# Clearing semaphores ahead of the final wait of a transfer-bound kernel, and letting that wait subtract

## Chip, cores, metric

The kernel runs on one core of one Trainium2 chip. The metric is the device time of one execution in microseconds (us). Each kernel was also executed once under the profiler, which leaves a trace. The *span* is the time from the first to the last instruction of that trace, and the measured time of the same execution is a little longer.

## The reference

```python
def reference(x, y):               # both 1024 x 4096, float32
    z = x * y
    return (0.5 * z * (1 + np.tanh(np.sqrt(2 / np.pi) * (z + 0.044715 * z ** 3)))).astype(np.float32)
```

A product and a GELU, element by element. 33.55 MB come in and 16.78 MB go out, so there are 50.33 MB to move for two passes of arithmetic.

## The kernel before

Everything is laid out as 128 partitions x 32768 columns. VectorE multiplies in place in `xs`, ScalarE applies the GELU in place, and the Sync engine (SP) issues all seven transfers and closes the program. Only this closing part is changed.

```python
    sem_x = [nc.alloc_semaphore(f"sem_x{i}") for i in range(len(X_LOADS))]    # 2
    sem_y = [nc.alloc_semaphore(f"sem_y{i}") for i in range(len(Y_LOADS))]    # 3
    sem_o = [nc.alloc_semaphore(f"sem_o{i}") for i in range(len(STORES))]     # 2
    sem_mul = nc.alloc_semaphore("sem_mul")
    sem_act = nc.alloc_semaphore("sem_act")
    # ... (loads, multiplications, activations cut)
    for i, (a, b) in enumerate(STORES):                # (0, 16384), (16384, 32768)
        nc.sync.wait_ge(sem_act, b // STEP)
        nc.sync.dma_start(out=out_r[:, a:b], in_=xs[:, a:b]).then_inc(sem_o[i], 16)
    for i in range(len(STORES)):
        nc.sync.wait_ge(sem_o[i], 16)
    nums = sorted(s.num for s in [*sem_x, *sem_y, *sem_o, sem_mul, sem_act])
    assert nums == list(range(nums[0], nums[-1] + 1))
    nc.sync.sem_clear(range(nums[0], nums[-1] + 1))
```

A *semaphore* is a counter: a transfer or an engine raises it, and a wait holds an engine until it has reached a value. The clear puts all nine back to zero at once, so that the next execution can count from there, and before the change it comes after both waits.

Of the kernel before, what the change touches and what calls it, by code (L numbers as in the profile page):

```python
# [1 line left out]

# [4 lines left out]


F32 = mybir.dt.float32
GELU = mybir.ActivationFunctionType.Gelu_apprx_tanh  # L10


X_LOADS = [(0, 16384), (16384, 32768)]

Y_LOADS = [(0, 16384, 0), (16384, 24576, 0), (24576, 32768, 8192)]
STEP = 4096
STORES = [(0, 16384), (16384, 32768)]
Y_RING = 16384


def _hoist(nc, issued):

    here = nc.cur_bb.bb.instructions
    first = nc.main_func.blocks[0].instructions
    for ins in issued:
        del here[next(k for k, i in enumerate(here) if i is ins or i.name == ins.name)]
    engine = issued[0].engine
    at = next(
        k
        for k, i in enumerate(first)  # L30
        if i.engine == engine and type(i).__name__ == "InstDrain"
    )
    first[at:at] = issued


@with_exitstack
def kernel(
    ctx: ExitStack,
    tc: tile.TileContext,
    x: bass.AP,  # L40
    y: bass.AP,
    out: bass.AP,
):
    nc = tc.nc
    P = nc.NUM_PARTITIONS

    x_r = x.flatten_outer_dims().rearrange("(p a) c -> p (a c)", p=P)
    y_r = y.flatten_outer_dims().rearrange("(p a) c -> p (a c)", p=P)
    out_r = out.flatten_outer_dims().rearrange("(p a) c -> p (a c)", p=P)
    total_f = x_r.shape[1]  # L50


    tc.close()
    tc.compile()  # L54

    xs = nc.alloc_sbuf_tensor("xs", [P, total_f], F32).ap()
    ys = nc.alloc_sbuf_tensor("ys", [P, Y_RING], F32).ap()
    sem_x = [nc.alloc_semaphore(f"sem_x{i}") for i in range(len(X_LOADS))]
    sem_y = [nc.alloc_semaphore(f"sem_y{i}") for i in range(len(Y_LOADS))]
    sem_o = [nc.alloc_semaphore(f"sem_o{i}") for i in range(len(STORES))]  # L60
    sem_mul = nc.alloc_semaphore("sem_mul")
    sem_act = nc.alloc_semaphore("sem_act")

    def load_x(i):
        a, b = X_LOADS[i]
        return nc.sync.dma_start(out=xs[:, a:b], in_=x_r[:, a:b]).then_inc(sem_x[i], 16)  # L66

    def load_y(i):
        a, b, r = Y_LOADS[i]
        return nc.sync.dma_start(  # L70
            out=ys[:, r : r + b - a], in_=y_r[:, a:b]
        ).then_inc(sem_y[i], 16)

    _hoist(nc, [load_x(0).ins, load_y(0).ins])
    load_x(1)
    for i in (1, 2):
        nc.sync.wait_ge(sem_mul, (Y_LOADS[i][1] - Y_LOADS[1][0]) // STEP)
        load_y(i)

    n = 0  # L80
    for i, (a, b, r) in enumerate(Y_LOADS):
        for j, (xa, xb) in enumerate(X_LOADS):
            if xa <= a < xb:
                nc.vector.wait_ge(sem_x[j], 16)
        nc.vector.wait_ge(sem_y[i], 16)  # L85
        for c in range(a, b, STEP):
            nc.vector.tensor_mul(  # L87
                out=xs[:, c : c + STEP],
                in0=xs[:, c : c + STEP],
                in1=ys[:, r + c - a : r + c - a + STEP],  # L90
            ).then_inc(sem_mul, 1)
            n += 1
            nc.scalar.wait_ge(sem_mul, n)
            nc.scalar.activation(  # L94
                out=xs[:, c : c + STEP], in_=xs[:, c : c + STEP], func=GELU
            ).then_inc(sem_act, 1)

    for i, (a, b) in enumerate(STORES):
        nc.sync.wait_ge(sem_act, b // STEP)
        nc.sync.dma_start(out=out_r[:, a:b], in_=xs[:, a:b]).then_inc(sem_o[i], 16)  # L100
    for i in range(len(STORES)):
        nc.sync.wait_ge(sem_o[i], 16)
    nums = sorted(s.num for s in [*sem_x, *sem_y, *sem_o, sem_mul, sem_act])
    assert nums == list(range(nums[0], nums[-1] + 1))
    nc.sync.sem_clear(range(nums[0], nums[-1] + 1))


# [1 line left out]
_INS = ['x', 'y']  # L109
_OUTS = [((1024, 4096), 'float32')]  # L110


# [23 lines left out]
```

## Time and profile before

| | before |
|---|---|
| measured, first three runs | 120.77 to 120.79 us, median 120.79 |
| measured, the profiled execution | 120.85 us |
| its span | 119.535 us |
| measured minus span, same execution | 1.315 us |
| last increment of the last store's semaphore | 119.415 us |
| from there to the end of the span (the **tail**) | 0.120 us |

Values with three decimals are from the single records of the trace; the views round them to one or two.

The prediction below shows the views that carry the argument. One more belongs here: the busy times of the kernel before by stage. The columns are the stretch, its length, the busy us of VectorE, ScalarE and POOL with the number of instructions, the granted clock, the busy share of the DMA engines and GB/s.

```profile
58.80:80.80 22.00, 8.76 (x2) 8.77 (x3) 0.00 (x0) 1.00 1.03 429
80.80:93.30 12.50, 8.76 (x2) 9.31 (x3) 0.00 (x0) 1.00 0.97 419
93.30:119.50 26.20, 0.00 (x0) 0.00 (x0) 0.00 (x0) 1.00 0.92 400
```

The last row: no engine computes for 26.2 us and only the two stores run (the first lands at 100.1 us, the last at 119.4). Whatever the Sync engine does in that stretch *before* the last store has landed lies beside it. Whatever it does *after* is added.

### The profile page before, as it was taken

The numbers are of one execution on the slowest core, as the hardware profiler recorded it, in microseconds if no ns is written. First come the engines' busy times: TensorE is split into PE (matmuls) and PEld (weight loads), VectorE is DVE, ScalarE is ACT, GpSimd is POOL, SyncE is SP. The second block draws the span as 40 slices with busy tenths as digits, with TensorE's granted clock in tenths as the row PEclk, the third lists the DMA queues.
The fourth block names the chain that finished last, engine by engine and source line by source line (L and its number), as shares of the span: only waits on it lengthen the run. The fifth ranks groups of instructions, "written<-read, shape, count | busy, mean of one in ns | idle before, by whom it ended". The sixth has DMA issues, their size and how long they took to land.

```text
span 119.5 us, 68 instructions
## 1 busy us (share of the span) xinstructions
DVE 35.0 (29%) x8; ACT 30.2 (25%) x9; POOL 0.2 (0%) x4
## 2 busy tenths in 40 slices
DVE  0000000000000199999600049959990000000000
ACT  3000000000000006797780000977479200000000
POOL 0000000000000000000000000000000000000000
DMA  9889888998899889988898989998899888988890
GB/s 351 351 373 680 351 351 351 636 417 351 351 636 417 351 351 526 526 351 351 351 526 351 504 373 482 395 526 351 351 395 658 351 351 351 702 351 351 351 680 22
DMA packets 1008, 50.33 MB, mean 421 GB/s; under 512 B 112, under 2 KB 112, under 8 KB 112
## 3 DMA queue, kind: packets, MB, share of 16 engines
q1 hardware_dynamic: 1008, 50.33, 98.5%
HBM read 33.55 MB, written 16.78 MB: 421 GB/s over the span
## 4 chain that ended last, share of the span: by engine, by line
DMA 53%; DVE 22%; ACT 3%; SPq 0%; issue 0%; DVEq 0%
DMA ys<-in_y_dram 53%; DVE xs L87 22%; ACT xs L94 3%; SPq L66 0%; DVEq L85 0%
## 5 line engine op out<-in xcount | busy, mean ns | idle before, releaser
L87 DVE TENSOR_TENSOR xs<-xs,ys 128x4096 f32<-128x4096 f32 x8 | 35.0, 4421 | 54.7 <-DMA ys<-in_y_dram 54.7
L94 ACT ACTIVATE xs<-xs 128x4096 f32<-128x4096 f32 x8 | 28.9, 3617 | 61.1 <-DVE xs L87 61.1
L94 ACT ACT_TABLE_LOAD x1 | 1.3, 1283 | 1.9 <-PEq L54 1.9
L120 POOL MEMSET const-bfloat16-1.0<- 128x1 bf16 x1 | 0.1, 102 | 0.0
L120 POOL MEMSET const-uint8-127<- 128x1 uint8 x1 | 0.1, 102 | 0.0
L120 POOL MEMSET const-float32-1.0<- 128x1 f32 x1 | 0.1, 99 | 0.0
L120 POOL MEMSET const-float32-0.0<- 128x1 f32 x1 | 0.1, 98 | 0.2 <-issue 0.2
## 6 DMA issues: line engine op xcount, KB each, us to landing
ys<-in_y_dram SPq DMA_DIRECT2D x2, 4096.0 KB, 21.1
xs<-in_x_dram SPq DMA_DIRECT2D x2, 40.3
out_dram<-xs SPq DMA_DIRECT2D x2, 31.9
ys<-in_y_dram SPq DMA_DIRECT2D x1, 40.8
```

The lines of the kernel that those rows point to most:

```text
L87: nc.vector.tensor_mul(out=xs[:, c : c + STEP], in0=xs[:, c : c + STEP], in1=ys[:, r + c - a : r + c - a + STEP],).then_inc(sem_mul, 1)
L94: nc.scalar.activation(out=xs[:, c : c + STEP], in_=xs[:, c : c + STEP], func=GELU).then_inc(sem_act, 1)
L120: nc = _bacc.Bacc("TRN2", target_bir_lowering=False, num_devices=1)
```

## The change

Its intent is to have less left to do when the last store lands: clear the eight semaphores that are done with while that store still runs, and let the final wait put its own semaphore back to zero.

```diff
-    sem_o = [nc.alloc_semaphore(f"sem_o{i}") for i in range(len(STORES))]
     sem_mul = nc.alloc_semaphore("sem_mul")
     sem_act = nc.alloc_semaphore("sem_act")
+    sem_o = [nc.alloc_semaphore(f"sem_o{i}") for i in range(len(STORES))]
@@
-    for i in range(len(STORES)):
+    for i in range(len(STORES) - 1):
         nc.sync.wait_ge(sem_o[i], 16)
-    nums = sorted(s.num for s in [*sem_x, *sem_y, *sem_o, sem_mul, sem_act])
+    nums = sorted(s.num for s in [*sem_x, *sem_y, *sem_o[:-1], sem_mul, sem_act])
     assert nums == list(range(nums[0], nums[-1] + 1))
     nc.sync.sem_clear(range(nums[0], nums[-1] + 1))
+    nc.sync.wait_ge(sem_o[-1], 16).then_inc(sem_o[-1], -16)
```

The compiled program has two closing instructions either way. Before: a wait for the second store, then a clear of nine that also carries the wait for the first store. After: a clear of eight that carries the wait for the first store, then one wait for the second store with a subtraction of 16.

## The prediction

> **What bounds the kernel now.** I read the page first, then the chain that ended last in order of time, then the waits of the DMA queue on the Sync engine (SP), and last the two closing lines of the kernel one by one, because they are all that the change touches.
>
> The page says that transfers fill the span. In part 2 the DMA row stands at 8 or 9 in every slice but the last, and in part 3 one queue holds 16 DMA engines for 98.5% of the span. VectorE (29%) and ScalarE (25%) have room to spare.
>
> ```profile
> span 119.5 us, 68 instructions
> ...
> DVE  0000000000000199999600049959990000000000
> ACT  3000000000000006797780000977479200000000
> ...
> DMA  9889888998899889988898989998899888988890
> ...
> q1 hardware_dynamic: 1008, 50.33, 98.5%
> ```
>
> Here 50.33 MB in 119.5 us is 421 GB/s. VectorE and ScalarE have their last 9 in slice 30 or 31, about 90 us in; from there to the end the kernel is one store draining.
>
> The chain by time agrees: loads, multiplications, loads, multiplications, and a last activation that ends at 89.68 + 3.62 = 93.30 us. Its printed end is that last piece of computing, not the end of the span, so a second view is needed for the remaining 26.2 us. The waits of the Sync queue fill it:
>
> ```profile
> engine line waited for: us in total, times, longest us
> SPq L70 <- DVE xs L87: 56.2, 2, 47.9
> SPq L100 <- ACT xs L94: 33.8, 2, 30.5
> SPq L102 <- DMA out_dram<-xs: 25.8, 1, 25.8
> ```
>
> The third line is the one to see: the wait of line 102 sits for 25.8 us on the last store and is over only with it. What comes after that wait is on the path of everything, and it is two instructions:
>
> ```profile
> L102 SPq EVENT_SEMAPHORE  x1: 17/17/17, 119.4 to 119.4; - x1
> ...
> L105 SPq EVENT_SEMAPHORE_RANGE_CLEAR  x1: 40/40/40, 119.5 to 119.5; - x1
> ```
>
> The columns are shortest, middle and longest duration in ns, then the start in us. The records of the trace behind these lines carry three decimals: the sixteenth and last increment of the last store's semaphore is at 119.415 us, the wait of line 102 starts at 119.431 and lasts 0.017, the clear starts at 119.495 and lasts 0.040, and that is the end of the span, 119.535 us. So from the landing to the end of the span there are 0.120 us, and nothing else is in them. That is the whole stake of this change.
>
> **What the Trainium skill says.** "Perfetto Trace Analysis", section "Sequencer-only Instruction (DRAIN, etc)": the profiler reports only the execution of such an instruction; its wait for a semaphore and the spreading of its own update are not in the reported window. The trace agrees: line 102 is printed as 17 ns though it waited 25.8 us. So I work with starts and not with durations alone: the step from the wait to the clear is 119.495 - 119.431 = 0.064 us, of which only 0.017 is printed.
>
> "DMA: Bandwidth & Descriptors", section "Why a DMA increments its semaphore by 16 and not by 1": each engine that takes part adds 1 after its own data, and only the full 16 means that all has landed. The trace has 16 increments of the last store's semaphore, from 118.962 to 119.415 us. So subtracting 16 at that moment leaves exactly zero, what the clear left before, and the increments cannot be cut across by the early clear, since that semaphore is now outside its range.
>
> The same page, section "Anatomy of one DMA — SWDGE (gpsimd) path", puts most of the fixed cost of a transfer (about 2 us there, for the other way of issuing) into waiting for the confirmation of the write. Here the last data packet ends at 119.065 and the last increment comes at 119.415, 0.35 us later. That is much less than the page's figure, and in any case the change leaves it as it is.
>
> "Runtime: NRT & Kernel Launch", section "The ~15µs preamble/postamble breakdown", lists work of the runtime after the kernel. No record of the trace shows any of it; I only see that the measured 120.79 us is about 1.25 us more than the span of 119.535, and I assume that this part follows the end of the Sync engine and keeps its size.
>
> **The change part by part.** (1) The first wait loop loses its last turn. The compiled instruction lists show that the wait for the first store never was an instruction of its own: before, it rides on the clear. After, it still rides on the clear, which now stands alone in front. Instructions removed: none; SP has 7 listed rows in both.
>
> (2) The clear moves ahead of the final wait. It now starts when the first store has landed. That store was issued at 62.45 us and took 37.7 us (the longer of the two landing times of line 100), so 62.45 + 37.7 = about 100.1 us. All loads, multiplications and activations are over by then (last activation 93.30, last store issued 93.3), so nobody needs the eight semaphores any more. Its 0.040 us lie inside the 25.8 us of waiting for the second store, with 119.4 - 100.1 = 19.3 us of slack. Cost on the path: zero.
>
> (3) The final wait gains a subtraction. Waits with a subtraction are already in the trace: two of POOL's four in line 54, and POOL's first in line 120. They are printed as 17 ns, the same as the bare wait of line 102:
>
> ```profile
> L54 POOLq EVENT_SEMAPHORE  x4: 17/17/17, 1.4 to 1.8; - x4
> ```
>
> In its records POOL's wait with subtraction starts at 1.073 us and the next instruction at 1.152, a step of 0.079 against 0.064 from the bare wait to the clear. So the update may cost 0.015 us after the printed window.
>
> (4) The semaphores are allocated in another order (the stores' last), so that the range to clear stays contiguous without the last one; the clear then covers 8 instead of 9. It costs nothing on the path either way.
>
> Sum for the span: landing 119.415, start of the final wait 0.016 later as before, 0.017 of execution, end at 119.448 instead of 119.535. That is **0.087 us** less, which is the 0.064 step to the clear plus its 0.040 minus the 0.017 that the wait itself still takes. For the measured time I take off the 0.015 of a slower step after a subtraction: 0.087 - 0.015 = 0.072, and the middle of the two is 0.08. 120.79 - 0.08 = **120.71 us**, 0.07% faster.
>
> **The rivals.** *The saving vanishes behind the end of the program.* If the 1.25 us outside the span wait for something other than SP's last instruction, or start at the landing anyway, the time stays 120.79. For it: I cannot see that stretch. Against it: the other four engines have nothing recorded after 93.30 us, so they cannot be the late ones. About 1 in 5.
>
> *The clear costs more than it prints.* Clearing nine semaphores may hold the sequencer beyond the 0.040 us, just as the bare wait occupied 0.064 for a printed 0.017. Then the saving is larger: if the clear's step exceeds its window by the same 0.047, 0.064 + 0.087 - 0.079 = 0.072 by steps, and every further hidden 0.05 would come on top, giving about 120.62 to 120.66. About 1 in 5.
>
> *The subtraction is dear.* A read-modify-write of a semaphore that DMA engines have just written might be slower than POOL's in the preamble. Twice the 0.079 step would bring the time back to 120.79. I see nothing for it beyond the 0.015; 1 in 10.
>
> *The transfers shift.* A clear at 100 us, in the middle of the last store, could disturb it only if it touched that store's semaphore, which it does not. The stream itself may wander: the three timed runs lie within 0.02 us, but the profiled execution took 120.85. This gives the range its width and not the middle.
>
> **Range and chances.** The middle is 120.71. Below it the second rival reaches about 120.62; above it the first and third end at 120.79; a shift of the stream of a few hundredths, as between 120.79 and 120.85, widens both ends: 120.60 to 120.82. A change of 2% would be 2.4 us, and all that follows the last landing inside the span is 0.12 us, so a faster verdict would need twenty times the stake. Slower by 2% would need a disturbed stream. Chances: faster 0.003, same 0.992, slower 0.005.
>
> **What the profile of the changed kernel would show.** The clear of the Sync queue at about 100.1 us, 40 ns or slightly less, and no line of it at the end; the last Sync instruction is the wait, 17 ns, some 0.016 us after the last landing, and the span ends with it, near 119.45 us; the landing of the last store is unmoved near 119.4; engine work and DMA rows are the same. If the span falls by 0.09 and the measured time does not, the first rival is right. If the wait prints clearly more than 17 ns, the third. The prediction would be wrong if the landing of the last store itself moved by more than a tenth of a microsecond, or if the unseen end of the program grew or shrank with what SP does last.

## The result, and the profile after

| | before | after |
|---|---|---|
| median of six runs each, taken together | 120.87 us | 120.78 us |
| lowest to highest | 120.77 to 121.28 | 120.63 to 121.05 |
| ratio | | 0.999, 95% interval 0.997 to 1.001: the same |
| span of the profiled execution | 119.535 | 119.297 |
| last increment of the last store | 119.415 | 119.264 |
| tail | **0.120** | **0.033** |
| measured minus span, same execution | 1.315 | 1.333 |

A ratio is the mean time of one kernel's fast runs over the mean of the other's in the same rounds, so it is not quite the ratio of the medians quoted beside it.

The page of the changed kernel gives the same picture of transfers as before. These are its span, its DMA row and its DMA queue:

```profile
span 119.3 us, 68 instructions
...
DMA  9899888998899889988898989998889888998894
...
q1 hardware_dynamic: 1008, 50.33, 98.7%
```

The two closing lines of the changed kernel, each from the view of one source line (shortest, middle and longest duration in ns, then the start):

```profile
L105 SPq EVENT_SEMAPHORE_RANGE_CLEAR  x1: 45/45/45, 100.0 to 100.0; - x1
...
L106 SPq EVENT_SEMAPHORE  x1: 17/17/17, 119.3 to 119.3; - x1
```

The clear has left the end: it starts at 100.0 us, when the first store has landed. The last instruction is the wait, and it prints 17 ns with its subtraction, as the bare one did.

The waits of the Sync queue of the changed kernel hold a trap for readers:

```profile
SPq L100 <- ACT xs L94: 33.7, 2, 30.4
SPq L106 <- SPq L106: 19.3, 1, 19.3
SPq L105 <- DMA out_dram<-xs: 6.5, 1, 6.5
```

The 25.8 us before the end are now cut in two by the clear, 6.5 + 19.3 = 25.8. But the second part is put down to line 106 itself. The releaser is inferred from semaphore events, and the last event on this semaphore is now the subtraction of line 106. What really released it is the store: its sixteenth increment is at 119.264 us and the wait starts at 119.280. A wait that names itself is to be checked against the landings.

The span fell by 0.238 us, but only 0.120 - 0.033 = 0.087 of it belongs to the tail. The other 0.151 is the landing of the last store, 119.415 against 119.264. It was there before any changed instruction ran: the last load already landed 0.148 earlier, at 80.641 against 80.789 us. The repeats below show that this wanders.

### The profile page after: what moved, and what is told of

Read it like the earlier page. It is cut to its first block, busy times and chain, and to the rows that moved or that the text cites. A ratio compares the mean times of both kernels' runs of the same rounds, so it can differ in the third digit from the quotient of the medians.

```text
span 119.3 us, 68 instructions
## 1 busy us (share of the span) xinstructions
DVE 35.0 (29%) x8; ACT 30.2 (25%) x9; POOL 0.2 (0%) x4
## 4 chain that ended last, share of the span: by engine, by line
DMA 53%; DVE 22%; ACT 3%; SPq 0%; issue 0%; DVEq 0%
DMA ys<-in_y_dram 53%; DVE xs L87 22%; ACT xs L94 3%; SPq L66 0%; DVEq L85 0%
```

## The experiments

The theory: the stake is the time that the Sync engine needs after the last landing, and each of its instructions there counts in full. The rivals: the end of the program hides it; a clear or a subtraction costs more than it prints; clears beside a running store disturb it. Eleven runs were made, each on one chip and with runs of the kernel before beside it.

### The same two kernels again

No edit; five rounds each.

> The changed kernel once more, with more rounds. Theory: the tail from the last landing to the end of the span is 0.033 us again (0.120 in the kernel before), and the measured time lies 0.07 to 0.09 us below the kernel before, but single runs wander by 0.2 us with the landing of the last store, so the median may differ by anything from -0.3 to +0.15. Rival (the end of the program takes the saving back): measured time minus span is 0.087 us larger than in the kernel before (1.40 against 1.315). If the theory holds it is larger by at most 0.02.

> The kernel before against itself, to measure the noise. Ratio 1.000 with an interval about as wide as that of the change (0.997 to 1.001); tail 0.120 us; measured time minus span 1.315 us.

> The changed kernel a third time. Theory: tail 0.033 us, measured time minus span 1.33 to 1.34, that is 0.01 to 0.02 above the kernel before; measured time 0.07 below before, with single runs scattered over 0.4 us. Pooled over its three rounds of measuring the difference should come out between 0.0 and 0.2 us below before.

| | median | lowest to highest | ratio to before, 95% interval | landing | tail | measured - span |
|---|---|---|---|---|---|---|
| before again | 121.17 | 120.72 to 121.62 | 1.0012, 0.9992 to 1.0033 | 119.407 | 0.120 | 1.323 |
| after again | 120.80 | 120.61 to 121.02 | 0.9982, 0.9969 to 0.9995 | 119.238 | 0.034 | 1.338 |
| after, third time | 120.76 | 120.70 to 120.91 | 0.9991, 0.9978 to 1.0004 | 119.328 | 0.033 | 1.339 |

The tail repeats to 0.001 us, while the time of one and the same kernel wanders by 0.9 us from lowest to highest, ten times the effect. Measured minus span came out slightly above what was expected: 1.323 for 1.315, and 1.338 where at most 0.02 over the kernel before was allowed (0.023 over the first trace of it, 0.015 over the one of the same lot). With all runs of both kernels pooled, before has a mean of 120.96 us (43 runs, standard deviation 0.20) and after 120.81 (17 runs, 0.15). The difference is 0.155 us, with a standard error of 0.046 (the root of 0.20 squared over 43 plus 0.15 squared over 17), so 0.06 to 0.25. The 0.087 of the tail lies inside. The timed runs thus speak for a small gain but do not size it; the trace does.

The records also say where the wandering comes from: not from the closing part. In the 13 traces the last load lands anywhere between 80.617 and 81.193 us, but from there to the landing of the last store it is 38.610 to 38.636 us in eleven of them (the other two are taken up below). Counted from the landing of the last load, the span ends after 38.746, 38.750 and 38.749 us with the old closing (before, before again, and the renumbering below) and after 38.656, 38.655 and 38.665 with the new one, 0.090 less. The measured time of the same six executions, counted from the same point, is 40.061, 40.073 and 40.067 against 39.989, 39.993 and 40.004, 0.072 less.

### The renumbering alone

```diff
 # the kernel before
-    sem_o = [...]          # ahead of sem_mul and sem_act
+    sem_o = [...]          # behind them
```

> The kernel before with only the part of the change that allocates the stores' semaphores last. All theories: tail 0.120 us, measured time minus span 1.31 to 1.33, measured time that of the kernel before within noise (ratio 0.998 to 1.002).

Ratio 1.0007 (0.9991 to 1.0024), tail 0.120 us. The order of allocation is worth nothing in itself. Its profiled execution had its last store land at 119.822 us, 0.4 later than in the first trace of the kernel before: another look at how much the landing wanders without cause in the closing code (its last load had landed 0.404 later, too).

### Only the order of the two waits

```diff
 # the kernel before
-    for i in range(len(STORES)):
+    for i in reversed(range(len(STORES))):
         nc.sync.wait_ge(sem_o[i], 16)
```

> The kernel before with only the order of its two final waits turned round, so that the wait for the last store rides on the clear and the wait for the first store stands alone ahead. Theory: what matters is how many instructions stand behind the last landing: now one, a clear of 0.040 us, so the tail is 0.016 + 0.040 = 0.056 us, 0.064 less than before and 0.023 more than in the changed kernel. Rival (a clear must come after a wait of its own, or a wait on a clear reacts later): the tail stays near 0.12. Measured time 0.06 below before, within the noise of 0.2.

The two closing lines of this kernel, from the views of their source lines:

```profile
L102 SPq EVENT_SEMAPHORE  x1: 17/17/17, 100.1 to 100.1; - x1
...
L105 SPq EVENT_SEMAPHORE_RANGE_CLEAR  x1: 40/40/40, 119.4 to 119.4; - x1
```

The separate wait is now over at 100.1 us, and the clear itself waits for the last store. The tail is 0.056 us, 0.064 less than before, as the theory had it to the thousandth: what went is the step from a wait to the instruction behind it. Measured 120.90 us against 120.88, ratio 1.0004 (0.9992 to 1.0017), within the noise. So 0.064 of the 0.087 in the tail needs no subtraction and no second group of semaphores, only the order in which two waits are written.

### The subtraction undone

```diff
 # the changed kernel
-    nc.sync.wait_ge(sem_o[-1], 16).then_inc(sem_o[-1], -16)
+    nc.sync.wait_ge(sem_o[-1], 16)
+    nc.sync.sem_clear(range(sem_o[-1].num, sem_o[-1].num + 1))
```

> The changed kernel with the subtraction undone: the final wait is bare and a clear of that one semaphore follows, on which the wait rides. Theory: tail 0.016 plus one clear, 0.05 to 0.06 us, whether it clears one semaphore or nine. Rival (a clear's time goes with the number of semaphores): clearly below 0.040 for one semaphore, tail under 0.045. Measured time within noise of the changed kernel.

The wait rides on the clear of the one semaphore, so that again one instruction is left at the end:

```profile
L107 SPq EVENT_SEMAPHORE_RANGE_CLEAR  x1: 25/25/25, 119.6 to 119.6; - x1
```

The tail is 0.042 us, under the 0.05 to 0.06 of the theory, which missed here; the rival had it right. A clear of one semaphore prints 25 ns where the clear of nine at the end of the kernel before prints 40. That the time goes with the number is not shown, though: the early clear of eight prints 45, and an early clear of four, in the kernels with 64 waits below, 43. Measured 120.88 us, ratio 0.9995 (0.9981 to 1.0009). Of the 0.087, the subtraction itself is worth 0.042 - 0.033 = 0.009 over the next best closing. In the measured time counted from the last load's landing that does not show: 39.987 us here and 39.999 for the swapped waits, against 39.989 to 40.004 for the changed kernel.

### Many clears behind the end

```diff
 # the kernel before
-    nc.sync.sem_clear(range(nums[0], nums[-1] + 1))
+    for _ in range(1 + 64):
+        nc.sync.sem_clear(range(nums[0], nums[-1] + 1))
```

> The kernel before with 64 more clears behind its own. Theory: each clear is a step of 0.04 (its printed time) to 0.09 us (0.040 and the 0.047 by which a wait's step exceeds its printed time), all of it behind the landing and all of it in the measured time: 2.6 to 5.8 us more, in the span and in the measured time alike, 123.4 to 126.6 us. Rival (the end of the program hides what SP does last): the span grows by that much, the measured time by 1.3 us less. Rival (a clear costs much more than it prints): steps over 0.1 us, more than 6.4 us.

```profile
L106 SPq EVENT_SEMAPHORE_RANGE_CLEAR  x65: 38/38/63, 119.6 to 124.4; - x65
```

The tail grew from 0.120 to 4.956 us, by 4.836; the measured median went from 121.00 to 125.78, by 4.78 (by 4.85 for the profiled execution, counted from the last load's landing). Measured minus span was 1.338 us. **What the Sync engine does behind the last landing is paid in full**: the rival in which the end of the program takes it back is out. In the records, one clear follows the other at 0.068 us in the steady run of them, for a printed 0.038. The first two steps are 0.089 and 0.080, the last two 0.110 and 0.475. These last two return in other runs and are taken up below.

### Many subtracting waits behind the end

```diff
 # the changed kernel; sem_x and two of sem_y are taken out of the early clear
     nc.sync.wait_ge(sem_o[-1], 16).then_inc(sem_o[-1], -16)
+    four = [*sem_x, *sem_y[:2]]
+    for k in range(16):
+        for s in four:
+            nc.sync.wait_ge(s, 16 - k).then_inc(s, -1)
```

> The changed kernel with 64 more waits behind its last, each of them satisfied and subtracting 1 from a load's semaphore. Theory: a step of 0.079 us each, as POOL's in the preamble, so 5.1 us more than the changed kernel, in the span and in the measured time alike. Rival (subtraction is free behind the printed window): 0.064 us each, 4.1 us. Rival (subtraction is dear): over 0.1 us each, more than 6.4 us.

```profile
L110 SPq EVENT_SEMAPHORE  x64: 17/17/17, 119.8 to 124.4; - x64
```

The tail was 4.733 us, 4.700 more than in the changed kernel, and the measured median 125.62 against 120.88 for the kernel before. The steady step is 0.067 us, less than the 0.079 expected. Sixty-four such steps are 4.29 us, near the lower expectation, and the same two long steps at the end, here 0.104 and 0.441, add the other 0.41. So a subtraction is not dear. What it adds to a steady step is not shown, since no run has a row of bare waits. The step right behind the long wait, from the subtracting final wait to the first of the 64, is 0.088, against 0.064 from the bare wait to the clear in the kernel before.

### Many clears, and many waits, ahead of the final wait

```diff
 # the changed kernel
-    nc.sync.sem_clear(range(nums[0], nums[-1] + 1))
+    for _ in range(1 + 64):
+        nc.sync.sem_clear(range(nums[0], nums[-1] + 1))
```

> The changed kernel with 64 more clears ahead of the final wait. Theory: they lie in the 19.3 us of slack and cost nothing: same time as the changed kernel within 0.2 us, tail 0.033 us, landing of the last store at 119.2 to 119.5. Rival (clears beside a running store disturb it): the landing comes later by a microsecond or more.

This missed. The median was 121.70 us against 121.00 for the kernel before (ratio 1.0058, 1.0045 to 1.0071) and 120.80 for the changed kernel, 0.9 us more for work that should be hidden. The clears themselves did lie in the slack (100.5 to 104.9 us) and the tail was 0.034 as ever; the landing of the last store had moved, to 120.439 us. The page of this kernel has a line in its part 3 that none of the pages above has:

```profile
q1 hardware_dynamic: 1008, 50.33, 97.9%
q14 instruction: 1, 0.01, 0.0%
```

One packet of an instruction queue, 8,192 bytes, runs at 109.721 us for 0.309 us, in the middle of the store. The steps of the clears may mark where it was asked for: 0.110 instead of 0.069 at the last of them, at 104.9 us. That made two theories, told apart by half as many clears, and by as many instructions that are not clears.

```diff
-    for _ in range(1 + 64):                                # 64 clears
+    for _ in range(1 + 32):                                # shadow_32
```

```diff
 # the changed kernel: the 64 subtracting waits of the last experiment, ahead of the final wait   (shadow_waits)
+    for k in range(16):
+        for s in four:
+            nc.sync.wait_ge(s, 16 - k).then_inc(s, -1)
     nc.sync.wait_ge(sem_o[-1], 16).then_inc(sem_o[-1], -16)
```

> The changed kernel with 32 instead of 64 more clears ahead of the final wait. The 64 made the time 0.9 us longer against expectation. Theory A (the clears disturb the running store): half as many clears, half of it, about 0.45 us over the changed kernel. Theory B (the longer program makes the Sync engine fetch instructions once more, as one extra packet of an instruction queue at 109.7 us in that trace, in the middle of the store; the steps of 0.11 us near the last clears mark the place): 32 do not reach that place, no such packet, and the time is that of the changed kernel within 0.2 us.

> The changed kernel with 64 satisfied waits (each subtracting 1 from a load's semaphore) in place of the 64 clears ahead of the final wait. Theory A (clears disturb): no extra clears, so the time of the changed kernel within 0.2 us. Theory B (instruction fetch): the program is as long as with 64 clears, so one packet of the instruction queue during the store, and 0.5 to 1.2 us more.

| ahead of the final wait | measured | instruction packet in the store | issue of last store to landing | tail |
|---|---|---|---|---|
| 1 clear (after, third time) | 120.76 | none | 26.1 | 0.033 |
| 33 clears | 120.76 | none | 26.1 | 0.034 |
| 64 subtracting waits and 1 clear | 121.33 | one, at 109.329 | 26.5 | 0.033 |
| 65 clears | 121.70 | one, at 109.721 | 26.8 | 0.034 |

The first three rows were measured in one lot, the fourth in an earlier one. The landing times are the shortest of the two stores in the view of the issuing line. For 33 clears, 64 waits and 65 clears these are:

```profile
DMA to landing us min/median/max: 26.1/31.9/37.8
```

```profile
DMA to landing us min/median/max: 26.5/32.2/38.0
```

```profile
DMA to landing us min/median/max: 26.8/32.4/38.1
```

Thirty-two more clears cost nothing in time. Sixty-four further instructions of either kind do, and both times one instruction packet runs in the store. In the two kernels with as many instructions *behind* the end, the packet comes at 125.0 us, after the store, and the store lands at 119.486 and 119.669, within what the others show. So the length of the program alone does not make the loss.

Neither theory is the whole of it, as the single packets of the store show. Its data packets carry 65,536 bytes, and in the ten traces without extra instructions ahead of the final wait every one of them that starts after 93.0 us lasts 2.418 us; the early clear of the changed kernel lengthens none. In the three kernels with extra instructions, longer packets appear on one of the 16 DMA engines and on no other. (The trace does not name the engine; it is told by each packet starting where the one before it ended, to 0.004 us.) How much later that engine ended its part of the store, in us:

| ahead of the final wait | by longer store packets, nearly all while the instructions ran | by the instruction packet (0.309) and the longer packet right behind it (0.27) | together | its head start on the last of the other engines | left over |
|---|---|---|---|---|---|
| 33 clears | 0.30 | none | 0.30 | 0.59 | nothing |
| 64 subtracting waits and 1 clear | 0.14 | 0.58 | 0.72 | 0.45 | 0.27 |
| 65 clears | 0.67 | 0.58 | 1.25 | 0.67 | 0.58 |

The head start is what the engine would have had without the delays. So clears beside a running store do slow it, about in proportion to their number, as theory A had it; but they slow one engine, and 33 of them stay within its head start. The instruction packet of theory B runs on that same engine, and with it the head start is used up. The last increment of the store then came 0.467 and 0.471 us after the last data packet, against 0.331 to 0.351 in the other eleven traces. With that, the landing is 0.39 and 0.71 us late, counted from the last load's landing (39.011 and 39.339 us against 38.610 to 38.636).

The Trainium skill ("Runtime: NRT & Kernel Launch", section "Instruction fetch mechanics") describes how each sequencer, the part of an engine that runs its instructions, fetches them in blocks of 16 KiB by transfers of its own, and calls the cost of crossing a block boundary "mostly hidden". The trace agrees that there is such a transfer, though the packet has 8,192 bytes and that a boundary is crossed here is inferred. The cost is hidden from the sequencer, which is waiting anyway, but not from the store: in a kernel whose DMA engines are the bound the time was 0.57 us (121.33 against 120.76) and 0.90 us (121.70 against 120.80) longer, of which the fetch is a part.

What stays open: the remaining 0.2 us between the landings of the profiled executions and these medians; why the instructions slow one DMA engine (the profiler's own recording of them is not excluded); and whether the long steps near the end of each run of 64 belong to that fetch. The first of them, 0.104 to 0.110, ends at the 65th closing instruction in all four kernels; the second, 0.441 and 0.475, at the 66th in two, and in the other two the 66th is the final wait, which hides it.

## Why the prediction was right or wrong

**What bounds the kernel and what is at stake: right.** The transfers are unchanged, and all that the change could touch was the 0.120 us tail. The repeats with 0.120 and the 64 clears that were paid in full both show it.

**Parts 1 to 3, the cost on the path: right.** The prediction had the wait starting 0.016 us after the landing and lasting 0.017, and 0.087 us less behind the landing. The trace has 0.016, 0.017 and 0.087, three times over to 0.001. The span itself ended at 119.297 and not at 119.448, because the landing moved. The early clear was free, as said; it started at 100.0 us (said: about 100.1), but printed 45 ns where "40 ns or slightly less" was forecast. The renumbering, part 4, was free as well.

**The 0.015 for a slower step after a subtraction: supported, not settled.** Measured minus span is 1.333, 1.338 and 1.339 for the changed kernel against 1.315, 1.323 and 1.318 for the three traces with the old closing, on average 0.018 more. An estimate from steps, that is from start to start, says the same. The step behind the very last instruction is not recorded, so it is taken from the rows of 64: the old closing takes 0.064 + 0.068 and the new one 0.067 with steady steps, 0.064 + 0.089 and 0.088 with the steps right behind a long wait, so 0.065 us less either way and not 0.087. The measured gain, counted from the last load's landing, is 0.072, which is the prediction's 0.087 - 0.015. But the kernel with 33 clears ends in the same subtracting wait and has a measured minus span of only 1.319.

**The rivals.** The end of the program does not hide the gain; about 0.018 of it seems to go back. (The prediction's 1.25 us for that stretch mixes two executions; in one and the same it is 1.315.) The clear does cost more than it prints (steps of 0.068 to 0.089 for 0.038 to 0.048), but so does the wait that takes its place as last instruction (0.067 to 0.088 for 0.017), so the surplus takes some of the gain instead of adding to it. The prediction's own sum for this rival said so: it announces a larger saving and computes 0.072, less than 0.087. The subtraction is not dear. As to the transfers, "could disturb it only if it touched that store's semaphore" is wrong: 65 clears that do not touch it slowed a DMA engine by 0.67 us. The single clear of the change did not, and the shift that counted for the measured time lies ahead of the last load's landing.

**The width: too small.** The range, 120.60 to 120.82, held the median of 120.78 and the later ones of 120.80 and 120.76, but two of the six runs were outside (121.00 and 121.05), and so were five of the eleven later ones of the changed kernel. The weak step is the term for the stream, "a shift of the stream of a few hundredths". It was read from three runs within 0.02 us and a profiled one, and measured over 43 runs of the kernel before it has a standard deviation of 0.20 us. That the medians fell inside is in part luck: the same 0.08 taken off the mean of those 43 runs, 120.96, is 120.88, outside the range. For the same reason the prediction's own alarm went off falsely: the landing did move by more than a tenth (0.151), and yet nothing was wrong with the mechanism. "Same" never depended on it: 2% is 2.4 us.

## What to carry to other kernels

Read the end of a kernel from the last landing on: what the closing engine does behind it is paid for, at about 0.07 us for each instruction in these runs, whatever the profile prints for it, and what can be done ahead of the final wait should be. Here the order of two waits got most of it, since a wait can ride on the instruction behind it. A gain of this size is shown by the trace, in the distance from landing to end, and not by the clock; where the time wanders, look for an earlier event from which it no longer does (here the landing of the last load). Moving work into a wait is free only as long as it does not slow the transfer that is waited for: one clear did not, 33 slowed one DMA engine within its head start, and 64 further instructions, with a fetch of instructions in the middle of the store, went beyond it.

## What the Trainium skill lacked or had wrong

- "Runtime: NRT & Kernel Launch", section "Instruction fetch mechanics", calls the cost of a block boundary mostly hidden. With 64 more Sync instructions ahead of the final wait, one packet of 8,192 bytes ran in the last store and held up its DMA engine by 0.58 us; together with store packets that the instructions slowed on the same engine, the time rose by 0.57 and 0.90 us. What such a packet does to a running transfer is not on that page.
- "Perfetto Trace Analysis", section "Sequencer-only Instruction (DRAIN, etc)", says that waiting and the update are outside the printed window but gives no sizes. Here, on Sync: a bare wait prints 0.017 us and the next instruction starts 0.064 us after it; a subtracting wait 0.017 and 0.067 in a steady run, 0.088 behind a long wait; a clear of nine semaphores 0.038 to 0.048 in most cases, with a step of 0.068 in a steady run; a clear of one prints 0.025, of four 0.043, of eight 0.045.
- "DMA: Bandwidth & Descriptors", section "Anatomy of one DMA — SWDGE (gpsimd) path", has about 2 us of fixed cost per transfer, most of it the write receipt, for transfers issued from GpSimd. For the last store here, issued from Sync, the last increment came 0.35 us after the end of the last data packet (119.065 to 119.415 us; 0.331 to 0.351 in eleven traces, 0.47 in the two with an instruction packet in the store). It is another way of issuing, so this adds a size and contradicts nothing.
- No page names a releaser that the profile infers wrongly: a wait that changes its own semaphore is listed as released by itself (19.3 us, line 106), though the store released it.
